# Two small table loads, two loads of x and eight row loads of x, moved to other slots and another queue

## The chip, the cores and the metric

The kernel runs on one core of one Trainium2 chip. The metric is the device time of one execution in microseconds (us). Five engines work side by side, each on its own queue of instructions: PE (TensorE, matmuls), DVE (VectorE), ACT (ScalarE), POOL (GpSimd) and SP (SyncE, which only issues transfers). A transfer can be issued by SP, ACT or POOL; its data is moved by 16 DMA engines that all queues share. In the profile, q1 is the DMA queue of SP, q10 that of ACT and q0 that of POOL.

## The reference, cut to what matters

Two layers of a trunk for 256 rows of 2048 channels, in fp32. Each layer takes the RMS norm of x, multiplies it with one wide input projection, feeds the parts to two branches (a gated causal convolution of width 31 with a layer norm, and a multi-head latent attention with rotary positions), merges the branches through sigmoid gates, projects and adds x:

```python
def hybrid_layer(x, cos, sin, norm_g, w_in, ...):
    h = rmsnorm(x, norm_g)
    proj = h @ w_in
    (c_a, c_glu, c_gate, q_down, kv_down, k_pe, m_gate, g_conv, g_mla) = split(proj)
    y_conv = conv_branch(c_a, c_glu, c_gate, ...) @ w_proj_conv
    y_mla = mla_branch(q_down, kv_down, k_pe, m_gate, cos, sin, ...) @ w_proj_mla
    y = sigmoid(g_conv) * y_conv + sigmoid(g_mla) * y_mla
    return x + y @ w_out
```

For the change three inputs of the first layer count. The weights `w_in` and x itself, turned so that channels lie on partitions, feed the first matmuls. The sum of squares of every row of x gives the factor of the RMS norm; the kernel applies it behind the matmul, when a block leaves PSUM, so it isn't needed at the start. The tables cos and sin come from `positions` and 32 inverse frequencies and are needed later still.

## The kernel before, in words

**Products.** Every fp32 operand is split into a high part that PE takes exactly and a low rest, and a product is three matmuls: high by high, low of x by high, high of x by low. Weights come in pieces of 256 input channels for one block of up to 512 output columns. A piece is loaded into a `raw` tile (five buffers), ACT copies it into its high part (`hi`), DVE subtracts to get the low part (`lo`), and PE runs twelve matmuls on it: two halves of the rows, two groups of 128 channels, three products. Loads run four pieces ahead of the split, the high split three pieces and the low split two pieces ahead of PE.

**The first blocks.** In layer 0 the first four blocks (320, 384, 512 and 384 columns wide, in the order in which their pieces come) begin together: their pieces for the first 256 channels, then for the next 256, and from then on block by block. The first two pieces are loaded in halves of 128 channels each, to let PE begin early; the third piece, 512 columns wide, is the first whole one. x comes turned, in pairs of 128 channels (`load_x`, tile `x_in`, 256 KB a pair). `first_h` scales a tile of x by the norm's gain and splits it into `h_hi` and `h_lo`; a piece of weights needs the two tiles of x of its channels. Before that, 17 warm-up matmuls run on zeros.

**Slots.** The program is written out by a planner: after the matmuls of each piece, `background` counts a slot on and writes the steps that are due. `at_slot(n, f)` puts a step n slots after the one in which it is called. A slot is a place in the program text and no time on the chip: each engine goes through its own instructions in the order in which they were written (class `InOrder` adds an order with no wait), and between engines only data, and buffers that come free, hold an instruction back. All operations are recorded by one helper, so the profile gives line 143 for nearly all; tiles tell them apart.

**What the change touches.**

- `rope_tables` (line 591) is a generator. Up to its first `yield` it issues two loads on GpSimd's queue: the inverse frequencies, spread to all partitions (`invf_t`, 16 KB), and the positions (`pos_t`, 1 KB). Between the first and the second `yield` it does nothing. Then come small steps on DVE that build the angles, from slot 5 on. `rope_table_steps` (line 1453) drives it.
- The loop behind the first loads (line 583) puts x's pairs into SyncE's queue at slots 2 to 9. In that queue they stand between the weight loads, and those wait for free `raw` buffers.
- `first_sums` (line 658): `begin` loads x as rows into tiles `xres` (128x512, 256 KB each) from a pool with six buffers, and `end` lets ACT square and sum each of them (`junk`). Four calls, two tiles each; `begin` stands at slots 9, 10, 11 and 14, `end` at 13, 13, 14 and 17. `sum_x` at slot 18 makes the norm's factor `rinv_x` of the eight sums.
- On GpSimd's queue, behind the table loads, the next instruction in the program is a memset of the margin of `u_t`. It is written where the first gated block leaves PSUM (`glu_evac`, line 1068), which is due six slots after that block's last piece. Behind it the queue carries the transfers that turn this block (`turn_d<-su`), the layer's constants and the gains that are read as rows (`down<-in_rows`, 576 KB).

Of the kernel before, what the change touches and what calls it, by code (L numbers as in the profile page):

```python
# [131 lines left out]
def trunk(ctx: ExitStack, tc: tile.TileContext, xT, x, g_in, pos, win, wuq, wukv, wpc, wpm, wo, cst, rows, invf, out):  # L132
# [19 lines left out]
    pe, vec, act, gps, sp = (InOrder(e) for e in (nc.tensor, nc.vector, nc.scalar, nc.gpsimd, nc.sync))  # L152
# [100 lines left out]
    def load(i):  # L253
        if i >= len(pieces) or i in loaded:
            return
        ap, n = pieces[i]
        loaded[i] = t = raw_p.tile([P, KS * n], F32, tag="raw", name=f"raw{i}")
        sp.dma_start(t, ap)
# [50 lines left out]
    def at_slot(ahead, f, vec=0.0, act=0.0, first=False):  # L309
        steps.insert(0 if first else len(steps), (clock[0] + ahead, (vec, act), f))  # L310
# [259 lines left out]
    def load_x(engine, a, b):  # L570
        engine.dma_start(x_in[:, a:b, :], xT[:, a:b, :])
# [8 lines left out]
    load(3)  # L580
    load_x(sp, 2, 4)
    load(4)
    for slot, a in ((2, 4), (4, 6), (6, 8), (7, 10), (8, 12), (9, 14)):
        at_slot(slot, lambda a=a: load_x(sp, a, a + 2))


# [71 lines left out]
    def first_sums(t, c):  # L658

        xts = []  # L660

        def begin():
            for a in (c, c + 1):
                xts.append(wide_p.tile([P, 512], F32, tag="w", name="xres"))
                sp.dma_start(xts[-1], x[t, :, a * 512 : (a + 1) * 512])

        def end():
            for a, xt in zip((c, c + 1), xts):
                junk = work.tile([P, 512], F32, tag="junk", name="junk")
                act.activation(junk, xt, AF.Square, accum_out=ss_x[:, t, a : a + 1])  # L670

        return begin, end


    for l in range(DEPTH):
# [776 lines left out]

        def rope_table_steps():
            tables = rope_tables()
            next(tables)
            next(tables)
            for slot in (5, 6, 7, 8, 15, 16, 17, *range(21, 32)):
                at_slot(slot, lambda: next(tables, None), 0.95)

# [2 lines left out]
        for kind, i, pl in planned:  # L1462
            if kind == "glu":
# [13 lines left out]
                if i == 0:  # L1477
                    if l == 0:
                        rope_table_steps()
                    downs = FIRST_DOWNS[l]  # L1480
                    products_together(
                        pl, uses_h, lambda i, t, ps: down_evac(i - 1, t, ps) if i else glu_evac(0, t, ps),
                        (at,) + downs * (EVAC_AT,), ((0.9, 2.2),) + downs * ((0.0, 1.0),),
                        homes=("acc", "acc") if l else ("s", "acc", "acc", "tp"),
                    )
                    if downs == len(DOWN_BLOCKS):
                        down_after()
                    continue
# [159 lines left out]
```

## Time and profile before

| | |
|---|---|
| median of 3 runs | 1786.59 us (1786.55 to 1786.8) |
| the profiled execution | 1786.36 us, its span 1784.6 us |
| busy in the span | PE 1777.9, DVE 1538.4, ACT 1295.4, POOL 551.7 us |
| granted TensorE clock | 0.999 of full speed |
| bytes moved | 463.39 MB, mean 260 GB/s |
| weight loads of `w_in`, 512 KB each | 4.7 us from issue to landing (median) |

In the order of time a row gives the start in us, the time spent in us, the engine, the operation, the tile written and the tiles read, the shapes and the count, and in brackets the idle time before it with what ended it. A letter q behind an engine's name marks its queue of DMA issues. In the rows by stretch the first two numbers are the stretch and its length; then come the busy time and the count of instructions of PE, PEld (the loading of stationary operands), DVE, ACT and POOL, the granted clock, the busy share of the DMA engines and GB/s. In the rows of a DMA queue stand the packets, the MB and the time that the packets took, as a share of the time of 16 engines; it can come to a little over 100%, since packets overlap and are counted by where they start.

### The profile page before, as it was taken

Reading aid. Unit: us, or ns where it says so; the run is one execution under the profiler, and the core shown is the slowest. Engines: PE = TensorE matmul, PEld = TensorE weight load, DVE = VectorE, ACT = ScalarE, POOL = GpSimd, SP = SyncE. Lnnn points to the kernel's source line nnn. Section 1 sums busy time; section 2 is a strip of 40 time slices with the busy share of each in tenths; the row PEclk is TensorE's granted clock in tenths of the full one; section 3 lists DMA queues with packets and bytes.
Section 4 is the critical chain, followed back from the end, with each engine's and each line's share of the span. In section 5 each row is a group of like instructions: output and inputs, shape, how many; then the busy total and the mean of one; then the engine's idle time right before and its main releaser. Section 6 shows DMA issues by size and latency. Waiting matters only on the chain.

```text
span 1784.6 us, 27089 instructions
## 1 busy us (share of the span) xinstructions
PE 1777.9 (100%) x8575; PEld 1575.3 (88%) x8575; DVE 1538.4 (86%) x2487; ACT 1295.4 (73%) x2398; POOL 551.7 (31%) x1014
## 2 busy tenths in 40 slices
PE   9999999999999999999999999999999999999999
PEld 8988888888888888888899888888888888888887
DVE  6999898898999998867669998989899999887674
ACT  6778888988877675745567788898888777676442
POOL 0155565642311110011421555565333111100210
PEclk9999999999999999999999999999999999999999
DMA  8887888887898996678887888788879899867785
GB/s 300 264 279 260 268 283 263 274 292 235 271 251 253 259 266 223 218 239 290 309 265 232 273 279 268 256 281 277 284 244 287 242 248 256 257 209 221 247 285 175
DMA packets 149311, 463.39 MB, mean 260 GB/s; under 512 B 24608, under 2 KB 31024, under 8 KB 149168
## 3 DMA queue, kind: packets, MB, share of 16 engines
q1 hardware_dynamic: 105280, 358.66, 61.5%
q0 software_dynamic: 43296, 102.47, 20.1%
q8 instruction: 67, 1.10, 0.3%
q14 instruction: 76, 0.62, 0.1%
q10 hardware_dynamic: 592, 0.54, 0.1%
HBM read 399.18 MB, written 44.04 MB: 248 GB/s over the span
## 4 chain that ended last, share of the span: by engine, by line
PE 98%; DMA 1%; DVE 0%; ACT 0%; SPq 0%; issue 0%; DVEq 0%
PE acc L143 95%; PE s L143 2%; PE o_ps L143 1%; DMA x_in<-in_xT 1%; DMA raw<-in_win 0%; DVE lo L143 0%; SPq L143 0%; ACT hi L143 0%; DVE xres L143 0%; ACT h_hi L143 0%; DVE h_lo L143 0%; DVE table_steps L143 0%; PE var L143 0%; PE mu L143 0%; DVE tables L143 0%
## 5 line engine op out<-in xcount | busy, mean ns | idle before, releaser
L143 ACT CAST hi<-raw 128x1024 fp32r<-128x1024 f32 (+3 forms) x682 | 694.2, 1027 | 374.6 <-PE acc L143 281.2
L143 DVE TENSOR_TENSOR lo<-raw,hi 128x1024 fp32r<-128x1024 f32 (+3 forms) x682 | 811.3, 1193 | 143.8 <-PE acc L143 98.7
L143 PE MATMUL acc<-hi,hT 128*128 128x512 f32 (+2 forms) x1728 | 400.8, 373 | 0.0
L143 PEld LDWEIGHTS acc<-hi,hT 128*128 128x128 f32 x1728 | 320.4, 189 | 39.8
L143 PE MATMUL acc<-hi,h_hi 128*128 128x512 f32 (+2 forms) x864 | 251.9, 373 | 1.5 <-ACT hi L143 1.3
L143 PE MATMUL acc<-hi,h_lo 128*128 128x512 f32 (+2 forms) x864 | 251.0, 373 | 0.0
L143 DVE SCALAR_TENSOR_TENSOR v_t<-u_t,cst,v_t 128x256 f32<-128x256 f32 x562 | 239.8, 479 | 2.1
L143 PE MATMUL acc<-lo,hT 128*128 128x512 f32 (+2 forms) x864 | 220.3, 373 | 0.0
L143 PE MATMUL acc<-lo,h_hi 128*128 128x512 f32 (+2 forms) x864 | 220.3, 373 | 0.0
L143 PEld LDWEIGHTS acc<-hi,h_hi 128*128 128x128 f32 x864 | 160.7, 190 | 22.6 <-ACT hi L143 3.2
L143 PEld LDWEIGHTS acc<-hi,h_lo 128*128 128x128 f32 x864 | 161.7, 189 | 20.4
L143 PEld LDWEIGHTS acc<-lo,hT 128*128 128x128 f32 x864 | 161.2, 189 | 20.3
L143 PEld LDWEIGHTS acc<-lo,h_hi 128*128 128x128 f32 x864 | 161.2, 189 | 20.3
L143 POOL DMA_DIRECT2D turn_d<-gate x176 | 95.8, 552 | 231.5 <-DVE gate L143 157.4
L143 POOL DMA_DIRECT2D taps<-taps x70 | 61.3, 876 | 295.3 <-ACT taps L143 231.4
L143 ACT ACTIVATE taps<-u_t,cst 128x256 f32<-128x256 f32 x292 | 128.4, 498 | 0.4 <-DMA taps<-taps 0.4
L143 PE MATMUL acc<-hi,ycT 128*128 128x512 f32 x512 | 122.3, 379 | 0.0
L143 PE MATMUL acc<-hi,oT 128*128 128x512 f32 x512 | 122.3, 379 | 0.0
L143 PE MATMUL acc<-hi,yT 128*128 128x512 f32 x512 | 122.0, 379 | 0.0
L143 POOL DMA_DIRECT2D turned<-turn_d x88 | 49.9, 573 | 206.7 <-ACT hi L143 69.8
L143 PE MATMUL acc<-hi,qkc 128*128 128x512 f32 x448 | 110.5, 379 | 0.0
L143 PEld LDWEIGHTS acc<-hi,oT 128*128 128x128 f32 x512 | 97.0, 190 | 13.5
(187 smaller groups left out, 2360.6 us busy)
## 6 DMA issues: line engine op xcount, KB each, us to landing
raw<-in_win SPq DMA_DIRECT2D x384, 512.0 KB, 4.7
raw<-in_wpm SPq DMA_DIRECT2D x64, 512.0 KB, 5.0
raw<-in_wpc SPq DMA_DIRECT2D x64, 512.0 KB, 4.2
raw<-in_wo SPq DMA_DIRECT2D x64, 512.0 KB, 5.2
taps<-taps POOLq DMA_DIRECT2D x70, 256.0 KB, 6.4
raw<-in_wukv SPq DMA_DIRECT2D x32, 512.0 KB, 4.4
turned<-turn_d POOLq DMA_DIRECT2D x56, 256.0 KB, 5.8
raw<-in_wuq SPq DMA_DIRECT2D x24, 512.0 KB, 4.6
```

The lines of the kernel that those rows point to most:

```text
L143: ins = getattr(self.engine, name)(*a, **k)
```

## The change

```diff
@@ -580,7 +580,7 @@
     load(3)
     load_x(sp, 2, 4)
     load(4)
-    for slot, a in ((2, 4), (4, 6), (6, 8), (7, 10), (8, 12), (9, 14)):
+    for slot, a in ((2, 4), (4, 6), (6, 8), (7, 10), (7, 12), (8, 14)):
         at_slot(slot, lambda a=a: load_x(sp, a, a + 2))
 
 
@@ -662,7 +662,7 @@
         def begin():
             for a in (c, c + 1):
                 xts.append(wide_p.tile([P, 512], F32, tag="w", name="xres"))
-                sp.dma_start(xts[-1], x[t, :, a * 512 : (a + 1) * 512])
+                gps.dma_start(xts[-1], x[t, :, a * 512 : (a + 1) * 512])
 
         def end():
             for a, xt in zip((c, c + 1), xts):
@@ -1452,8 +1452,8 @@
 
         def rope_table_steps():
             tables = rope_tables()
-            next(tables)
-            next(tables)
+            at_slot(2, lambda: next(tables))
+            at_slot(3, lambda: next(tables))
             for slot in (5, 6, 7, 8, 15, 16, 17, *range(21, 32)):
                 at_slot(slot, lambda: next(tables, None), 0.95)
 
```

The first two calls of the generator are written at slots 2 and 3 rather than ahead of the first piece. The loads of x's channels 12 and 13 (in tiles of 128) go to slot 7, behind those of 10 and 11, and the loads of 14 and 15 to slot 8. The eight loads of x's rows are issued by GpSimd and no longer by SyncE, at the same slots as before. Nothing else is changed: the same bytes are loaded into the same tiles.

## The prediction

> **What bounds the kernel now.** I read the page's head and its chain of waits first, then the busy time in stretches, then the order of time of each engine over the first 60 us, because the three edits touch that stretch alone.
>
> ```profile
> span 1784.6 us, 27089 instructions
> PE 98%; DMA 1%; DVE 0%; ACT 0%; SPq 0%; issue 0%; DVEq 0%
> ```
>
> ```profile
> 4.56:10.56 6.00, 4.62 (x24) 3.55 (x24) 2.60 (x7) 2.99 (x6) 0.00 (x0) 1.00 0.93 307
> 10.56:33.91 23.35, 23.29 (x120) 21.04 (x120) 18.45 (x39) 14.16 (x23) 0.00 (x0) 1.00 0.89 304
> 60.00:1779.60 1719.60, 1719.60 (x8259) 1521.24 (x8259) 1493.15 (x2378) 1255.62 (x2330) 544.17 (x997) 1.00 0.82 259
> ```
>
> The second column is PE's busy time. From 60 us to 1779.6 us PE never stops, so a delay of PE before that is carried to the end one for one, and only a shorter or longer start can change the time. PE stands still in two places: 1.38 us in all between 4.56 and 10.56 (6.00 - 4.62), and a little in the next 23 us. Here are PE's rows and those of ScalarE, which splits the weights ahead of it.
>
> ```profile
> 0.78 3.67 PE L143 MATMUL warm<-const-float32-0.0 128*128 128x256 f32 x17 [0.78 <-PEq L1637]
> ...
> 10.56 0.70 PE L143 MATMUL acc<-hi,h_hi 128*128 128x512 f32 x2
> ...
> 12.39 1.03 PE L143 MATMUL acc<-lo,h_hi 128*128 128x512 f32 x4
> 13.26 0.49 PE L143 MATMUL acc<-hi,h_hi 128*128 128x384 f32 x2
> ...
> 32.83 1.03 PE L143 MATMUL acc<-lo,h_hi 128*128 128x512 f32 x4
> 33.91 0.70 PE L143 MATMUL acc<-hi,h_hi 128*128 128x512 f32 x2
> ```
>
> ```profile
> 6.86 0.46 ACT L143 CAST hi<-raw 128x320 fp32r<-128x320 f32 x1 [1.34 <-DMA raw<-in_win]
> 8.18 0.51 ACT L143 CAST hi<-raw 128x384 fp32r<-128x384 f32 x1 [0.87 <-DMA raw<-in_win]
> 9.47 1.82 ACT L143 CAST hi<-raw 128x1024 fp32r<-128x1024 f32 x2 [0.77 <-DMA raw<-in_win]
> ...
> 32.02 0.91 ACT L143 ACTIVATE h_hi<-x_in,gx 128x256 fp32r<-128x256 f32 x2 [1.70 <-DMA x_in<-in_xT]
> ...
> 36.98 0.63 ACT L143 ACTIVATE junk<-xres 128x512 f32<-128x512 f32 x1
> ```
>
> Three casts in a row wait for a load of weights, the last until 9.47. Of its row's two casts the first (of 1.82/7 x 4 = 1.04 us, by width 1024 to 768) ends at 10.51, and PE goes on at 10.56. So **the third piece of weights starts PE's unbroken run, with no slack**; every microsecond by which that load lands later is a microsecond of the kernel. The piece behind it has its cast done at 11.29 (9.47 + 1.82) and is used at 13.26: it has 1.97 us to spare. At 32.02 ScalarE waits for a pair of x's tiles, and PE then begins at 33.91, 1.08 us after its previous group, where the same group of four took 0.87 us earlier (12.39 to 13.26): 0.21 us lost.
>
> **Part 1: the small table loads, to slots 2 and 3.** A slot orders the program text; each engine is held to its own order only, and otherwise to data. GpSimd's rows show what a slot is worth there:
>
> ```profile
> 1.28 0.70 POOL L143 DMA_DIRECT2D invf_t<-in_invf  x1 [0.84 <-POOLq L1637]
> 1.98 0.55 POOL L143 DMA_DIRECT2D pos_t<-in_pos  x1
> 2.52 0.17 POOL L143 MEMSET u_t<- 128x60 f32 x1
> 51.92 4.37 POOL L143 DMA_DIRECT2D turn_d<-su  x8 [49.23 <-DVE su L143]
> ...
> 60.04 0.53 POOL L143 DMA_DIRECT2D down<-in_rows  x1
> ```
>
> The memset of u_t is written into the program with the first block's evacuation, some twenty slots in, and ran at 2.52 us, straight behind the position load; the engine then idled 49.23 us until data came. So a GpSimd instruction that waits for nothing runs at once, whatever its slot. Both table loads are issued by the first call of the generator (the second call issues nothing), nothing stands ahead of them in GpSimd's queue in slots 0 to 2, and they need no data: they stay at 1.28 and 1.98. Cost and gain **0**. If a slot did hold them, the rival below has the price.
>
> **Part 2: x's last two pairs one slot sooner.** SyncE's queue really is held, since the weight loads in it wait for free buffers.
>
> ```profile
> 13.04 0.42 SPq L143 DMA_DIRECT2D x_in<-in_xT  x1
> ...
> 22.77 0.42 SPq L143 DMA_DIRECT2D x_in<-in_xT  x1
> ...
> 26.70 0.43 SPq L143 DMA_DIRECT2D x_in<-in_xT  x1
> ...
> 29.87 0.42 SPq L143 DMA_DIRECT2D x_in<-in_xT  x1
> 30.35 0.90 SPq L143 DMA_DIRECT2D xres<-in_x  x2
> ...
> 39.32 1.16 SPq L143 DMA_DIRECT2D xres<-in_x  x2
> ```
>
> The pair now issued at 26.70 goes right behind that of 22.77, at 23.2, and the one at 29.87 takes the place at 26.70: 3.5 and 3.2 us sooner, against a wait of 1.70 us at 32.02. They are moved past one weight load each, whose issue comes 0.42 us later; that piece is used about three pieces on, so this stays hidden. Gain: the **0.21 us** at 33.91. Bounds: 0 if something else is late by then, 0.3 at most.
>
> **Part 3: eight row loads of x, from SyncE's queue to GpSimd's.** Now they are issued from 30.35 to 39.32, behind weight loads. In GpSimd's queue they stand behind the two table loads and ahead of the memset. The buffers (six, tag "w") are unused until then, so the first six loads wait for nothing. The price of one such issue on GpSimd, and the DMA side:
>
> ```profile
> L143 POOL DMA_DIRECT2D x_dram<-xres x8: 557/562/566, 853.9 to 899.7; - x8
> ```
>
> ```profile
> q0 software_dynamic: 33, 0.01, 57.2%
> ...
> q1 hardware_dynamic: 577, 1.34, 84.1%
> ...
> DMA packets 766, 2.05 MB, mean 410 GB/s; under 512 B 82, under 2 KB 95, under 8 KB 766
> q1 hardware_dynamic: 766, 2.05, 103.2%
> ...
> q0 software_dynamic: 188, 0.68, 74.0%
> q1 hardware_dynamic: 132, 0.31, 26.2%
> ```
>
> The rows are DMA totals by queue (q0 is GpSimd's, q1 SyncE's; the last number is the share of the 16 engines) in the stretches 4 to 5, 5 to 9.47, 7 to 12 (two rows) and 62 to 65 us. Six issues of 0.56 us run from 2.53 to 5.9. The loads that GpSimd issued from 1.28 keep the engines busy from 4 us on (57.2%), some 2.7 us later, so the first x rows move at about 5.0. Six loads of 256 KB are 1.573 MB, at 410 GB/s **3.84 us of all 16 engines**, and the engines have no such room: SyncE's weights take 84.1% of 5 to 9.47 and all of 7 to 12. These are the weights on which PE's run starts.
>
> How the queues share is the unknown. The nearest row is the stretch 62 to 65, in which a GpSimd load of 576 KB (issued at 60.04) met SyncE's weights and took 74.0% against 26.2%. By it the burst lasts 3.84/0.74 = 5.19 us, to 10.19, and SyncE's queue does 0.26 x 5.19 = 1.35 us of the 0.841 x 4.47 = 3.76 us of work that lands the third piece; the other 2.41 us bring that to 12.60 instead of 9.47, a delay of 3.13 us. Equal halves give 5.0 + 2 x 3.76 = 12.52, about the same. Upper bound: all 3.84 us ahead of the weights. Lower bound: GpSimd's queue gets a third, as its 2 KB rows stand to 4 KB rows of the weights (512 and 1024 fp32 a partition): 5.0 + 3.76 x 1.5 = 10.64, a delay of 1.17 us. I take **3.1 us**, by the row of 62 to 65.
>
> The Trainium skill speaks here in "DMA: Bandwidth & Descriptors", section "Queues, rings and completion order": each DMA engine takes turns between the queues that have work, a packet at a time, and the section "Issuing engines are not separate DMA queues" adds that another issuing engine brings no bandwidth. Turn by turn and with packets of one row the sum would be that of the lower bound, +1.0 us. The row of 62 to 65 stands against such even turns.
>
> The later pieces are delayed by at most 3.84 us and have 1.97 us or more to spare, so they add nothing to a shift of 3.1. What SyncE's queue is freed of after 30 us helps nobody: PE waits there for nothing but the pair already counted. The seventh and eighth row loads wait for the first two buffers, whose squares begin at 36.98; behind them on GpSimd stand the memset and the work of 51.92, more than ten microseconds off.
>
> **Sum.** 0 - 0.2 + 3.1 = +2.9 us. The profiled execution took 1786.36 us, its span of 1784.6 and 1.8 around it; the median of the runs is 0.23 above it. So 1786.36 + 2.9 + 0.23 = **1789.5 us**.
>
> **Rivals.** Two of them need the queues' shares of 4 to 7 us:
>
> ```profile
> q1 hardware_dynamic: 306, 0.45, 62.9%
> q0 software_dynamic: 63, 0.02, 22.5%
> ```
>
> **The clock falls.** In the forecast PE has finished its first half pieces near 7 us, and the next cast, now at 6.86, comes near 9.5 (62.9% of the 1.86 us from 5.0, worked off at 26%), so PE would stand still about 3 us. The warm row shows PE's slow pace: 17 matmuls of 256 columns in 3.67 us, 0.216 us each, which is what 512 columns take later (0.87/4). If the pause brings that pace back for one to two stretches of 3.67 us, half of it is lost, 1.8 to 3.7 us; with 2.7 the time is 1792.2. Against it: the short waits now did not do it. The Trainium skill, "TensorE: Matmul & The Clock Gate", section "Part 1: The HAM clock gate", says that an idle window of about 3.4 us halves the clock; the pause forecast lies just under that, and no run yet shows it.
>
> **The slots do hold GpSimd** (the other side). The place is GpSimd's queue: tables at about 13.04, x's rows where they are now. Then q0's 22.5% of 4 to 7 us is free for weights, up to 0.68 us off the third piece; with the 0.2 of part 2: 1785.7 us. It decides if anything holds the loads past 9 us. The memset at 2.52 speaks against it.
>
> **The burst is hidden.** GpSimd's queue yields and its loads fill the 37% left before 7 us and the gaps after 12: delay 0.2, time 1786.6. The row of 62 to 65 speaks against it, the smaller rows of x for it.
>
> **Chances.** Forecast 0.57, clock 0.18, slots hold 0.08, hidden 0.17. The forecast's own range is 1787.6 to 1790.2, from the bounds 1.17 and 3.84 less 0.2. Less than 0.2% (3.6 us) can't be told from no change here. Over that lie nearly all of the clock's case and about a tenth of the forecast's: slower 0.24; faster by as much has no mechanism, 0.02; the rest, 0.74, within. The range takes in the hidden case and most of the clock's: 1786.3 to 1792.3.
>
> **What would show it.** Six xres issues back to back on GpSimd from about 2.5 us; q0 over half of the DMA between 5 and 10 us; the casts now at 6.86, 8.18 and 9.47 later by 2 to 4 us; PE's unbroken run begun near 13.7 rather than 10.56; no gap before the group now at 33.91. I am wrong if the xres issues come after 9 us, if the cast of 9.47 moves by less than 1 us, or if matmuls of 512 columns take 0.43 us after the pause.

## The result, and the profile after

| | before | after |
|---|---|---|
| median | 1786.59 us | 1789.31 us |
| lowest to highest of 22 runs each | 1785.6 to 1789.75 | 1788.07 to 1793.21 |
| ratio, 95% interval | | 1.0015 [1.0008, 1.0021] |
| profiled execution, span | 1786.36, 1784.6 us | 1789.25, 1787.4 us |

The change makes the kernel 2.7 us slower, with an interval of 1.4 to 3.75 us. The forecast was 1789.5 us. The sum came out, but its terms did not: the profile has three of them where the prediction had one. Of the twelve executions of `pairs_only` below, the profiled one ran at a granted clock of 0.948 and took 1858.03 us; it counts in the median and not in the ratio, and its trace is not used.

GpSimd and SyncE in order of time, of the changed kernel:

```profile
1.28 0.70 POOL L143 DMA_DIRECT2D invf_t<-in_invf  x1 [0.83 <-POOLq L1637]
1.97 0.55 POOL L143 DMA_DIRECT2D pos_t<-in_pos  x1
2.51 3.17 POOL L143 DMA_DIRECT2D xres<-in_x  x6
38.98 0.54 POOL L143 DMA_DIRECT2D xres<-in_x  x1 [33.29 <-ACT junk L143]
...
25.91 0.90 SPq L143 DMA_DIRECT2D x_in<-in_xT  x2
...
29.43 0.43 SPq L143 DMA_DIRECT2D x_in<-in_xT  x1
```

The table loads did not move. The six row loads left at once, from 2.51 to 5.7 us, and the seventh waited for the first buffer. ScalarE and PE of the same kernel show what that did:

```profile
7.00 0.46 ACT L143 CAST hi<-raw 128x320 fp32r<-128x320 f32 x1 [1.53 <-DMA raw<-in_win]
8.97 0.51 ACT L143 CAST hi<-raw 128x384 fp32r<-128x384 f32 x1 [1.52 <-DMA raw<-in_win]
10.93 1.04 ACT L143 CAST hi<-raw 128x1024 fp32r<-128x1024 f32 x1 [1.45 <-DMA raw<-in_win]
...
15.54 0.91 ACT L143 ACTIVATE h_hi<-x_in,gx 128x256 fp32r<-128x256 f32 x2 [0.97 <-DMA x_in<-in_xT]
...
31.25 0.91 ACT L143 ACTIVATE h_hi<-x_in,gx 128x256 fp32r<-128x256 f32 x2 [0.58 <-DMA x_in<-in_xT]
...
33.01 0.91 ACT L143 ACTIVATE h_hi<-x_in,gx 128x256 fp32r<-128x256 f32 x2
```

```profile
9.53 0.59 PE L143 MATMUL acc<-hi,h_hi 128*128 128x384 f32 x2 [1.49 <-ACT hi L143]
...
12.02 0.70 PE L143 MATMUL acc<-hi,h_hi 128*128 128x512 f32 x2 [0.70 <-ACT hi L143]
...
17.36 0.54 PE L143 MATMUL acc<-hi,h_hi 128*128 128x320 f32 x2 [0.52 <-ACT hi L143]
...
33.42 0.59 PE L143 MATMUL acc<-hi,h_hi 128*128 128x512 f32 x2
...
36.01 0.59 PE L143 MATMUL acc<-hi,h_hi 128*128 128x512 f32 x2
...
170.20 1.95 PE L143 MATMUL s<-qk_t 128*128 128x256 f32 x16
```

The third piece's cast is 1.46 us later (10.93 against 9.47) and so is PE's run (12.02 against 10.56). There is then a second stop that was not there before, at 17.36, when ScalarE has waited until 15.54 for x's pair 2 to 4 and splits the fifth piece only behind it. The group that began at 33.91 begins at 36.01, 2.59 us behind its predecessor, which is the twelve matmuls at full pace: the gap before it is gone. At the first scores of the attention the kernel is 2.0 us behind. Before, this row reads:

```profile
168.21 1.95 PE L143 MATMUL s<-qk_t 128*128 128x256 f32 x16
```

The third term lies far from the change. The chain of waits between 709 and 1057 us has these pieces, after:

```profile
709.44 93.25 PE acc L143 x432
...
804.03 6.54 DMA raw<-in_wo
...
815.40 241.78 PE acc L143 x1202
```

Between 802 and 815 us, where the output projection starts, PE loses another 0.9 us (the second layer's first scores come 2.88 us later than before, at 1057.44 for 1054.56). Before, that stretch was one unbroken piece of PE. Whether it belongs to the change is a question for the experiments.

The shares of the DMA queues in 5 to 9.47 us (first two rows) and in 7 to 12 us, after:

```profile
q1 hardware_dynamic: 449, 0.99, 57.8%
q0 software_dynamic: 185, 0.50, 34.9%
...
q0 software_dynamic: 303, 1.01, 53.2%
q1 hardware_dynamic: 366, 0.99, 50.1%
```

SyncE's weights got 57.8% instead of 84.1% of the first stretch and half of the second instead of all. Other stretches of the same trace say when the rows moved and how the queues shared: GpSimd's queue in 0 to 6 us and in 6 to 7 us (first two rows), both queues in 9 to 12 (two rows), GpSimd's in 14 to 15 (last row).

```profile
q0 software_dynamic: 60, 0.05, 15.8%
...
q0 software_dynamic: 32, 0.08, 27.8%
...
q0 software_dynamic: 208, 0.68, 60.2%
q1 hardware_dynamic: 209, 0.51, 44.2%
...
q0 software_dynamic: 27, 0.07, 17.6%
```

Up to 6 us GpSimd's queue moves 0.05 MB, tables included (0.02 MB before); nearly all of the rows' 1.573 MB comes after that, and the last of it just behind 15 us. In 9 to 12 us, where both queues have work, they move as many packets as each other, 208 and 209, and their shares of the time differ with the bytes, 0.68 and 0.51 MB.

### The profile page after: what moved, and what is told of

Same layout as the page of the kernel before. It is cut to its first block, busy times and chain, and to the rows that moved or that the text cites. A ratio compares the mean times of both kernels' runs of the same rounds, so it can differ in the third digit from the quotient of the medians.

```text
span 1787.4 us, 27086 instructions
## 1 busy us (share of the span) xinstructions
PE 1778.6 (100%) x8575; PEld 1572.2 (88%) x8575; DVE 1538.2 (86%) x2487; ACT 1294.3 (72%) x2398; POOL 553.3 (31%) x1022
## 4 chain that ended last, share of the span: by engine, by line
PE 98%; DMA 1%; DVE 0%; ACT 0%; issue 0%; DVEq 0%
PE acc L143 95%; PE s L143 2%; PE o_ps L143 1%; DMA x_in<-in_xT 1%; DMA raw<-in_wo 0%; DVE lo L143 0%; DMA gx<-in_g 0%; DVE yT L143 0%; DVE xres L143 0%; ACT hi L143 0%; ACT h_hi L143 0%; DVE h_lo L143 0%; PE var L143 0%; PE mu L143 0%; DVEq L143 0%
## 5 line engine op out<-in xcount | busy, mean ns | idle before, releaser
L143 PEld LDWEIGHTS acc<-hi,ycT 128*128 128x128 f32 x512 | 96.8, 189 | 13.7
```

The source lines that it names most:

```text
L143: ins = getattr(self.engine, name)(*a, **k)
```

## The experiments

The question is which part of the change costs the time, by what, and how much of the 2.7 us is chance elsewhere. The theory is the burst: six row loads at 2.5 us share the DMA engines with the first weights. The rivals are that the two other parts cost it, that GpSimd's queue is slow wherever it runs, and that the time is lost far behind the start.

**One part alone.** `rows_only` is the kernel before with this edit:

```diff
-                sp.dma_start(xts[-1], x[t, :, a * 512 : (a + 1) * 512])
+                gps.dma_start(xts[-1], x[t, :, a * 512 : (a + 1) * 512])
```

> Only the eight row loads go to GpSimd's queue; table loads and x's pairs as before. Theory (the burst): six loads issued from about 2.5 us, q0 over a third of 5 to 9.5 us, third piece's cast near 10.9 rather than 9.47, and a second stop of PE near 17 us for x's pair 2 to 4; PE is 2.0 to 2.5 us later at the first scores (168 us before), and the time is 2.3 to 3.2 us over before. Rival (parts 1 or 2 cost it): within 0.5 us of before.

Measured: 1789.29 us, ratio 1.0017 [1.0008, 1.0025], the same as the whole change. First scores at 169.40, 1.2 us late. So the rows carry the loss. The 2.0 us expected at the first scores were too much for this execution.

`pairs_only` and `pairs_again` are the kernel before with the loop of x's pairs alone changed:

```diff
-    for slot, a in ((2, 4), (4, 6), (6, 8), (7, 10), (8, 12), (9, 14)):
+    for slot, a in ((2, 4), (4, 6), (6, 8), (7, 10), (7, 12), (8, 14)):
```

> Only x's last two pairs a slot sooner. Theory: the 0.2 us at 33.91 are saved and nothing else changes, -0.2 us. Rival (part 2 delays the weight loads it is moved past): +0.5 us or more.

> Only x's last two pairs a slot sooner, for its trace. Theory: the start up to 31 us as before, ScalarE waits less than 0.5 us for these pairs, and the 0.2 us before the group that began at 33.91 are gone.

Measured: 1786.23 us, ratio 0.9995 [0.9986, 1.0004]: 0.2 us can't be told from nothing, but a loss of 0.8 us or more is excluded. In the trace of `pairs_again` ScalarE no longer waits for these two pairs:

```profile
29.29 0.90 ACT L143 ACTIVATE h_hi<-x_in,gx 128x256 fp32r<-128x256 f32 x2
...
31.03 0.90 ACT L143 ACTIVATE h_hi<-x_in,gx 128x256 fp32r<-128x256 f32 x2
```

`tables_only` is the kernel before with the two calls put into slots 2 and 3:

```diff
-            next(tables)
-            next(tables)
+            at_slot(2, lambda: next(tables))
+            at_slot(3, lambda: next(tables))
```

> Only the table loads' lines move to slots 2 and 3. Theory (a slot holds no GpSimd instruction that waits for nothing): both are issued at 1.3 and 2.0 us as before, the third piece's cast is at 9.3 to 9.6. Rival: they are issued near 13 us, the cast comes near 8 to 8.5.

Measured, GpSimd in order of time:

```profile
1.27 0.70 POOL L143 DMA_DIRECT2D invf_t<-in_invf  x1 [0.83 <-POOLq L1637]
1.97 0.55 POOL L143 DMA_DIRECT2D pos_t<-in_pos  x1
```

The loads stay where they were. The third piece's cast came at 9.06 us, a little under the expected 9.3, and in `pairs_again` at 8.67: with nothing moved ahead of it, this shows how far the start varies by itself.

**When, or by whom.** `held_rows` is the changed kernel in which the first three groups of row loads wait for VectorE; `held_both` holds the table loads too:

```diff
+                if a == c and (t, c) != (1, 2):
+                    vec.memset(xts[-1][:, :1], 0.0)
                 gps.dma_start(xts[-1], x[t, :, a * 512 : (a + 1) * 512])
...
+        vec.memset(invf_t[:, :1], 0.0)
         gps.dma_start(invf_t, invf.partition_broadcast(P))
```

> As the changed kernel, but each of the first three groups of row loads waits for a one-column memset that VectorE makes in its tile at the same slot, so that GpSimd issues them near 30 to 36 us. Theory (it is when they are issued, not by whom): the first 30 us are as before, and the time is 0.2 to 0.4 us under before. Rival (GpSimd's queue itself slows the weights wherever it runs): a stop of PE near 35 to 45 us and 1 to 3 us over before.

> As held_rows, and the table loads also wait for a memset at slot 2, so that they are issued near 13 us. If the table loads cost the first weights up to the 0.68 us of engine time that they take between 4 and 7 us: 0.5 to 0.7 us under held_rows, third piece's cast before 9.2. If their share was time that the weights could not use: no difference to held_rows.

Measured: `held_rows` 1787.0 us, ratio 1.0002 [0.9993, 1.001]; `held_both` 1787.5 us, 1.0001 [0.9992, 1.001]. Two rows of `held_rows`, GpSimd and PE:

```profile
30.42 1.06 POOL L143 DMA_DIRECT2D xres<-in_x  x2 [27.90 <-DVE xres L143]
...
51.94 0.92 PE L143 MATMUL acc<-lo,h_hi 128*128 128x384 f32 x4 [0.38 <-DVE lo L143]
```

The same loads, by the same engine, at 30 us instead of 2.5, and the loss is gone: the first scores come at 168.06 us (168.21 before), and the interval of the ratio reaches from 1.3 us under before to 1.8 us over it. What counts is when they run. The 0.2 to 0.4 us of gain that were expected are not there. PE stops near 51 us, a new place. `held_both` suggests why, in rows of GpSimd, ScalarE and PE:

```profile
12.21 0.70 POOL L143 DMA_DIRECT2D invf_t<-in_invf  x1 [11.76 <-DVE invf_t L143]
...
7.91 1.83 ACT L143 CAST hi<-raw 128x1024 fp32r<-128x1024 f32 x2 [1.18 <-DMA raw<-in_win]
...
39.05 0.63 ACT L143 ACTIVATE junk<-xres 128x512 f32<-128x512 f32 x1 [1.17 <-DMA xres<-in_x]
...
51.33 0.92 PE L143 MATMUL acc<-lo,h_hi 128*128 128x384 f32 x4 [0.37 <-DVE lo L143]
...
520.09 0.70 PE L143 MATMUL acc<-lo,h_hi 128*128 128x512 f32 x2 [1.66 <-DVE lo L143]
```

With the tables held, the third piece's cast comes at 7.91, 1.0 us sooner than in `held_rows` (8.88). So the two small loads do cost the first weights about a microsecond where they are. But ScalarE waits for the rows of x (39.05), VectorE makes the norm's factor of them just behind, and PE waits at 51.33 for a low part that VectorE writes only then. That is read from the order of time; no run tests it alone. At the first scores 0.6 us of the gain over `held_rows` is left (167.45 for 168.06), and a stop of 1.66 us at 520 takes it back in this execution.

`tables_held_pairs` leaves the rows with SyncE, holds the tables and moves x's pairs: the version that the experiments so far pointed to.

> Rows stay with SyncE as before; the table loads wait for a one-column memset of VectorE at slot 2, and x's last two pairs come a slot sooner. If the early table loads cost the first weights about 1 us (third piece's cast 7.9 to 8.5 us instead of 9.5) and nothing takes it back: first scores 0.8 to 1.4 us sooner than 168.2, time 0.7 to 1.5 us under before. Rival (what the start gains is given back where ScalarE waits for the rows of x and VectorE for the norm's factor, as near 51 us with the rows held): a stop of PE near 51 us and less than 0.5 us gained at the first scores.

Measured: 1786.47 us, ratio 0.9999 [0.999, 1.0008]. Its third piece's cast:

```profile
7.48 1.80 ACT L143 CAST hi<-raw 128x1024 fp32r<-128x1024 f32 x2 [0.75 <-DMA raw<-in_win]
```

That is 2.0 us sooner than in the first trace of before, and the first scores come 1.05 us sooner (167.16), with no stop near 51. But `pairs_again`, with the tables where they were, reached them at 167.08, so these traces show no gain at the first scores. In the times of its eleven runs the gain can't be seen; it beats the changed kernel, not the kernel before.

**How much of the burst.** `rows_two` and `rows_four` send two and four of the row loads by GpSimd and the rest by SyncE:

```diff
-                gps.dma_start(xts[-1], x[t, :, a * 512 : (a + 1) * 512])
+                (gps if (t, c) == (0, 0) else sp).dma_start(xts[-1], x[t, :, a * 512 : (a + 1) * 512])
```

(with `t == 0` as the condition for four).

> As the changed kernel, but only the first two of the eight row loads go to GpSimd's queue; the other six stay with SyncE at their slots. Theory (it is the bytes of the early burst): two loads are a third of the six that ran early, 1.3 us of the DMA engines; the third piece's cast comes 0.4 to 0.8 us later than without, PE is 0.3 to 1.0 us later at the first scores, and the time is 0.3 to 1.2 us over before. Rival (any early GpSimd load of rows costs the whole): over before by 2 us or more.

> As the changed kernel, but only the first four of the row loads go to GpSimd's queue. With two early loads the third piece's cast was at 10.7 us and there was no second stop; with six it was at 10.9 and 11.1. Theory (the third piece is delayed by the first loads alone, since the queues share and it is through before the later ones; these delay what comes behind it): cast at 10.6 to 11.1, with a second stop of at most 0.5 us between 15 and 18 us. Rival (the delay grows with all the bytes): cast as far between those of two and of six as chance allows, but the stop at 12 us longer than with two by 0.5 us or more.

Measured: `rows_two` 1787.16 us, ratio 1.0 [0.9992, 1.0009]; `rows_four`, one execution, 1787.12 us. PE's first group of the third piece in `rows_two` (first row) and in `rows_four`, and ScalarE's wait for x's pair in `rows_four`:

```profile
11.84 0.70 PE L143 MATMUL acc<-hi,h_hi 128*128 128x512 f32 x2 [0.69 <-ACT hi L143]
```

```profile
10.93 0.70 PE L143 MATMUL acc<-hi,h_hi 128*128 128x512 f32 x2
...
13.53 0.91 ACT L143 ACTIVATE h_hi<-x_in,gx 128x256 fp32r<-128x256 f32 x2 [0.52 <-DMA x_in<-in_xT]
```

Two loads delayed the third piece more than four did, so a dose was not shown; the 10.6 to 11.1 expected of the cast with four was 9.83. With two the cast (10.74) was later than expected, the first scores were as late as expected (169.16, 0.95 us behind before), and the expected 0.3 to 1.2 us over before do not show in the time. Two loads cost less than the whole in the runs. The second stop came with all six early and neither with two nor with four. From the third piece to the sixth PE takes 6.27 or 6.28 us in both traces of before, `pairs_again`, `tables_only`, `rows_two` and `rows_four`, but 6.78 in `rows_only` (stop at 16.63), 7.07 in the changed kernel (stop at 17.36) and 6.52 in its repeat, where the loss is spread.

`x24_first` is the changed kernel with x's pair 2 to 4 moved ahead of the fourth piece:

```diff
     load(2)
-    load(3)
     load_x(sp, 2, 4)
+    load(3)
```

> As the changed kernel, but x's pair 2 to 4 stands ahead of the fourth piece in SyncE's queue. In the changed kernel PE stops twice, at 12.02 for the third piece and at 17.36 for the fifth, whose split waits for this pair. Theory: the second stop (about 0.5 us) goes and the first stays; PE reaches the first scores 0.3 to 0.8 us sooner than in the changed kernel, time 2.0 to 2.5 us over before. Rival (the second stop is the weights' own lateness): a stop of the same size stays before 20 us.

Measured: 1790.75 us, ratio 1.0016 [1.0007, 1.0025]. ScalarE and PE:

```profile
15.91 0.83 ACT L143 CAST hi<-raw 128x768 fp32r<-128x768 f32 x1 [3.17 <-DMA raw<-in_win]
16.65 0.91 ACT L143 ACTIVATE h_hi<-x_in,gx 128x256 fp32r<-128x256 f32 x2
...
16.80 0.59 PE L143 MATMUL acc<-hi,h_hi 128*128 128x384 f32 x2 [1.15 <-ACT hi L143]
```

Here the theory failed. The pair no longer has to be waited for, but the fourth piece, put behind it, is waited for instead, and PE stops longer, 1.15 us. In these traces what stands behind the third piece is late, and the order only says what.

**Chance.** `after_again` and `before_again` are the two kernels unchanged, for second traces.

> The changed kernel once more, for its trace. Of its 2.8 us over the span of before, 2.0 were there at the first scores and 0.9 came near 802 us, at the start of the output projection. Theory: the early part is there again, 1.5 to 2.5 us. If the part at 802 is chance, it is gone or elsewhere; if it belongs to the change, it is there again.

> The kernel before once more, for its trace: the third piece's cast near 9.5 us, the first scores near 168 us, and between 168 us and the end the lengths that the first trace showed, or, if the stops in the middle are chance, one of up to 1 us.

Landmarks of PE in order of time, in us: the first matmul of the third piece, the first scores, and the span.

| kernel | third piece | first scores | span | scores to end |
|---|---|---|---|---|
| before | 10.56 | 168.21 | 1784.6 | 1616.4 |
| before_again | 10.47 | 168.35 | 1786.5 | 1618.2 |
| pairs_again | 9.77 | 167.08 | 1784.6 | 1617.5 |
| tables_only | 10.16 | 167.47 | 1783.8 | 1616.3 |
| rows_two | 11.84 | 169.16 | 1785.1 | 1615.9 |
| rows_four | 10.93 | 168.38 | 1785.3 | 1616.9 |
| rows_only | 11.58 | 169.40 | 1787.5 | 1618.1 |
| after | 12.02 | 170.20 | 1787.4 | 1617.2 |
| after_again | 12.22 | 169.97 | 1790.9 | 1620.9 |
| x24_first | 12.80 | 171.59 | 1792.6 | 1621.0 |
| held_rows | 9.98 | 168.06 | 1785.2 | 1617.1 |
| held_both | 9.14 | 167.45 | 1785.7 | 1618.3 |
| tables_held_pairs | 9.19 | 167.16 | 1783.7 | 1616.5 |

The early part is there again: the three traces with six early loads in the changed order (`rows_only`, `after`, `after_again`) reach the first scores at 169.86 on average, the four of the first rows of the table, with no early load but the two small ones, at 167.78. That is **2.1 us**, with a spread of about 1 us within each group. At the third piece the same groups are 1.7 us apart (11.94 and 10.24); the second stop adds 0.25 to 0.8 us in each trace. The rest of the kernel, the same in all, takes 1615.9 to 1621.0 us. `before_again` loses 1.8 us there and `after_again` 4.5 us against the first trace of before. So the 0.9 us near 802 are of the size that executions of one kernel differ by, and `after_again` has its loss elsewhere, at 520 us. Whether the change makes such stops more frequent was not settled: no two kernels have enough traces for that.

## Why the prediction was right, and where not

- **The slots.** Right. GpSimd issued the row loads back to back from 2.51 us, and the table loads did not move (`tables_only`). The memset of u_t that had run at 2.52 was the telling row. The rival that slots hold GpSimd falls.
- **The price of an issue and the bytes.** Six issues took 3.17 us (forecast 3.4). The loads met the first weights as forecast.
- **The delay of the third piece.** This step failed: "I take 3.1 us, by the row of 62 to 65". The third piece was 1.46 us late in the first traces and 1.7 between the groups, and the casts that were to come 2 to 4 us later came 0.14, 0.79 and 1.46 us later. Three parts of the term were wrong. First, nearly all of the rows moved not from "about 5.0" but from 6 us on, behind the tables in their queue, and they lasted to about 15 us and not to 10.19. Second, GpSimd's queue got not 74.0% but 34.9% of 5 to 9.47 us, and 53.2% of 7 to 12. The row of 62 to 65 was a bad neighbour, a single large load of long rows against a queue whose demand at that time was not known. Third, by the cast at 10.93 SyncE's queue had worked 54.3% of 5.93 us, 3.22 us since 5.0, so the 3.76 us were more than the third piece needed. The share alone does not explain the miss, since equal halves from 5.0 on gave about the same 3.1 in the prediction's own sum. The nearness to the lower bound of 1.17 is luck too: it took GpSimd's rows as packets half as large as those of the weights, and in 9 to 12 us they were not smaller (0.68 MB in 208 packets against 0.51 MB in 209). The Trainium skill's rule in "DMA: Bandwidth & Descriptors", section "Queues, rings and completion order" (turns between the queues, a packet at a time) fits this trace: 208 packets against 209 in 9 to 12 us, where both queues had work. In 62 to 65 us before, 188 stood against 132.
- **The later pieces.** Also wrong: "The later pieces ... add nothing to a shift of 3.1". With a shift of only 1.46 their 1.97 us to spare were not enough, since what stands behind the third piece is delayed for as long as the burst lasts, here to about 15 us. x's pair, the fourth and fifth piece stand there, and the second stop follows. In the two traces of before and after, PE is 2.25 us behind once the sixth piece begins (19.09 for 16.84). The two errors have opposite signs, and so part of one is made up by the other: 2.25 against 3.1.
- **x's pairs.** Right in kind. The 0.21 us at 33.91 are gone (2.3 to 2.0 us at the first scores), but the repeat of before had no such gap, so its worth is 0 to 0.2 us.
- **The sum.** +2.9 forecast, +2.7 measured, of which the traces show 2.1 at the start; the other 0.6 lie within the interval and are not explained. That the time came so near is luck: the working did not deserve it.
- **The clock.** The rival's condition was not met: PE stood still for 1.49 us before 9.53, and 2.10 us in the repeat, less than the 3 us foreseen, and the granted clock stayed at 1.00 from 8.5 to 13 us in both. That the burst would be hidden is excluded by `rows_only`.

## What to carry to other kernels

In a program that is ordered by slots, look for a dependent instruction before trusting a slot: an engine whose next instruction waits for nothing runs it at once, and moving a load to an idle engine's queue can move it to the start of the kernel, into the one stretch where the first operands fill the DMA engines. If it is to run later, give it something to wait for, as `held_rows` did. To size such a burst, ask when its first bytes move, behind what stands ahead in its own queue; for the share between queues use a row in which both are known to have work. When a burst delays the first operand, follow it also to those behind.

## What was not expected

The clock's fall, which was a rival for the start, appeared near 520 us. PE of `after_again`:

```profile
9.73 0.59 PE L143 MATMUL acc<-hi,h_hi 128*128 128x384 f32 x2 [2.10 <-ACT hi L143]
...
520.36 0.59 PE L143 MATMUL acc<-hi,h_hi 128*128 128x512 f32 x2
523.53 1.07 PE L143 MATMUL acc<-lo,h_hi 128*128 128x512 f32 x2 [2.58 <-DVE lo L143]
524.40 1.06 PE L143 MATMUL acc<-hi,h_lo 128*128 128x512 f32 x2
...
527.48 0.59 PE L143 MATMUL acc<-hi,h_hi 128*128 128x512 f32 x2
527.91 0.59 PE L143 MATMUL acc<-hi,h_lo 128*128 128x512 f32 x2
```

After 2.58 us without work two matmuls of 512 columns start 0.87 us before the next two (523.53 to 524.40), twice the usual 0.43 (527.48 to 527.91), for some 3.7 us. `x24_first` shows the same at the same place after 2.27 us (its PE row, then the stretches at the slow pace in `after_again` and in `x24_first`):

```profile
524.85 0.98 PE L143 MATMUL acc<-lo,h_hi 128*128 128x512 f32 x2 [2.27 <-DVE lo L143]
...
523.53:527.48 3.95, 3.95 (x10) 3.19 (x11) 3.95 (x9) 1.99 (x3) 0.00 (x0) 0.57 0.95 227
...
524.85:528.80 3.95, 3.95 (x10) 3.18 (x11) 3.95 (x9) 2.08 (x3) 0.11 (x1) 0.57 0.88 225
```

The granted clock is 0.57 in both stretches and 1.00 behind the first (527.5 to 531 us). After 1.66 us at 520 (`held_both`) and 2.10 us at 9.73 the pace stayed. The Trainium skill, "TensorE: Matmul & The Clock Gate", section "Part 1: The HAM clock gate", puts the fall behind an idle window of about 3.4 us; here pauses of 2.3 and 2.6 us sufficed. In `after_again` the stop costs 2.74 us (523.53 less 520.36 and the 0.43 of a pair) and the ten slow matmuls 1.8 us more, together the 4.5 us of that execution, more than the change itself. Near 520 us PE waits for the low parts of weights on VectorE. Of the thirteen traces of the table six have no stop there, five have one of 0.2 to 1.66 us, and these two have 2.27 and 2.58. With all six loads early it is none, 1.10, 2.27 and 2.58; whether the early rows lengthen it, and so make up the unexplained 0.6 us, is open.
